# A decoder step on one core: its startup rewritten, with half-size loads on two queues, sample rows over all partitions, and a pinned order

## The chip, the cores and the metric

The kernel runs on one core of one Trainium2 chip. The metric is device time in microseconds (us). Three timed runs of the kernel before gave 1955.08, 1953.29 and 1950.29 us, median 1953.29. One more execution was taken with the profiler, and its trace is what is read here. The engines are named as the profile names them: PE (TensorE matmul), PEld (its weight load), DVE (VectorE), ACT (ScalarE), POOL (GpSimd) and SP (SyncE, which here only issues DMAs). `ACTq`, `SPq` and `PEq` are the instruction queues of those engines.

## What is computed

One inference step of a hybrid decoder layer, for 256 prompt tokens and 64 sample tokens (8 sequences of 8) that share all weights. Everything is float32:

```python
h = rmsnorm(x) * norm_mix_w                     # x: 320 tokens x 2048
proj = h @ w_in                                 # q, k, v, gates of two branches
x = x + (sig(gate_a) * (mlstm(proj) @ w_branch_a)
         + sig(gate_b) * (gla(proj) @ w_branch_b)) @ w_out
h2 = rmsnorm(x) * norm_ffn_w
u, g = h2 @ ffn_w_up, h2 @ ffn_w_gate
x = x + (gelu(conv3(u)) * g) @ ffn_w_down
y = rmsnorm(x) * final_norm_w                   # and the new recurrent states
```

The change touches only the first line, and the part of the second that makes q and k of the first two GLA heads.

## The kernel before

All activations stand transposed, features on the 128 partitions and the 320 tokens along the free dimension, so that a product is `[256 columns of w]^T @ h^T` in two PSUM tiles of 128x320. The weights are the stationary operand. A float32 product is done in three passes of the type float32r: a weight block `raw` is split into `wh` (a rounded copy, ACT, line 69) and `wl = raw - wh` (DVE, line 70), the activation likewise into `hH` and `hL`, and `mm3` (lines 74 to 76) adds wh·hH, wh·hL and wl·hH. Weight blocks are 512 KB (four row tiles by 256 columns); the pool `ring` keeps four `raw` and three each of `wh` and `wl`, so the loads run ahead of PE by a few blocks. PSUM holds four tiles with the tag `big` (products) and four with the tag `mx` (all else).

The startup, lines 131 to 219, makes h^T. `x_load(c)` brings 512 columns of x, one DMA for the prompt rows (512 KB) and one for the 64 sample rows (128 KB). `x_chunk(c)` transposes four feature tiles of 128 by the identity on PE (three transposes each: two blocks of prompt tokens and one of sample tokens, line 153), and evacuates each to hH (ACT, line 154), hL (DVE, line 155) and xT (lines 158 and 160), a plain copy that is written to DRAM by POOL (line 161) for the residual later. The norm's weight `nmw` is multiplied in there. The norm's scale per token is not: `token_scale` (lines 163 to 176) makes it apart. ACT squares the rows of x, one instruction for each block of tokens, and sums them (line 168), DVE divides by 2048 (169), POOL raises to the power -1/2 (170), DVE spreads each column over 128 (`lh`, 174), PE transposes the spread columns (175), and DVE copies the result to `rstd_bc` (176), by which every product is scaled when it leaves PSUM (`evac_scaled`, line 129).

While the chunks arrive, PE already multiplies: the first products are q and k of two GLA heads (`gq_ps`, `gk_ps`), which use up all four `big` tiles. They go over the 16 feature tiles in four steps of four, one step for each chunk, 24 matmuls for gq and 24 for gk in a step, 192 together. Eight matmuls on a tile of ones (line 110) run ahead of everything. Three transposes of small vectors (`vrow`, lines 215 to 217) follow, and then the product of the gates and all the others.

The order of the instructions on each engine isn't that of the code: `schedule_with_timeline_sim=True` lets a scheduler place them, engine by engine, when the program is built. Each engine then works through its list in that order and waits at each instruction for what it needs. DMAs wait in the same way, on SP's and ACT's queues: each load shares one of eight semaphores with the load issued eight before it, and is not issued before that one has landed.

## Time and profile before

| | us |
|---|---|
| timed runs | 1950.29 to 1955.08, median 1953.29 |
| span of the profiled execution | 1950.9 |
| PE busy in it | 1930.5 |
| first transposes of x on PE | 5.16 |
| first product matmul | 9.75 |
| first matmul after gq, gk and the vrow transposes | 48.31 |

The table's last three lines are starts of rows of the timeline, counted from the start of the span. "Busy" counts an engine from the start to the modelled end of its instructions, also where matmuls lie close behind each other and overlap; a busy PE may still be working slowly, so the pace is read from the starts of its matmuls. In an answer on waits, a row names who waited, for what, and for how long in total, how often, and at the longest. A row of the windows gives, for each engine, busy us and the number of instructions, then PE's granted clock (1.00 is full speed), the share of the DMA engines that was busy and the GB/s.

### The profile page before, as it was taken

To read this page: it belongs to the slowest core of one execution; us is meant where nothing else is said; L and a number is where in the kernel's file an instruction comes from. 1 tells how busy PE (TensorE), PEld (TensorE's weight loads), DVE (VectorE), ACT (ScalarE), POOL (GpSimd) and SP (SyncE) were. 2 spreads that over 40 slices of the span, in tenths; PEclk is the share of its full clock that TensorE was granted. 3 is DMA by queue.
4 is the path that set the end of the run, shared out by engine and by line. 5 is a ranking of instruction groups with operands and counts; after the bars stand their busy time and mean duration, and the time that the engine had idled before them with its cause. 6 is when DMAs were issued, how large, how long until landed. Compare 5 with 4: busy or idle time off the path is not lost.

```text
span 1950.9 us, 32725 instructions
## 1 busy us (share of the span) xinstructions
PE 1930.5 (99%) x13190; PEld 1908.9 (98%) x13190; DVE 1107.0 (57%) x1658; ACT 811.4 (42%) x1096; POOL 332.6 (17%) x618
## 2 busy tenths in 40 slices
PE   9999999999999999999999999999999999999997
PEld 8999999999999999999999999999999999999997
DVE  5767787878644444445655545554554555455455
ACT  5445444556533333333343324333432443343245
POOL 4221413143100000002211101110210120011014
PEclk9999999999999999999999999999999999999998
DMA  7745656575655555556444444444444444444442
GB/s 235 196 130 172 200 167 205 164 218 150 200 156 149 147 150 151 151 152 205 149 146 154 147 149 151 152 152 151 143 151 151 151 152 151 151 148 150 148 151 95
DMA packets 300224, 311.63 MB, mean 160 GB/s; under 512 B 15264, under 2 KB 292026, under 8 KB 300073
## 3 DMA queue, kind: packets, MB, share of 16 engines
q1 hardware_dynamic: 287849, 283.53, 48.0%
q0 software_dynamic: 7328, 24.50, 3.7%
q8 instruction: 103, 1.69, 0.4%
q10 hardware_dynamic: 4896, 1.52, 0.3%
q14 instruction: 48, 0.39, 0.1%
HBM read 287.03 MB, written 22.48 MB: 159 GB/s over the span
## 4 chain that ended last, share of the span: by engine, by line


## 5 line engine op out<-in xcount | busy, mean ns | idle before, releaser
L70 DVE TENSOR_TENSOR wl<-raw,wh 128x1024 fp32r<-128x1024 f32 x504 | 628.1, 1246 | 623.3 <-ACT wh L69 621.5
L69 ACT ACTIVATE wh<-raw 128x1024 fp32r<-128x1024 f32 x504 | 533.9, 1059 | 852.2 <-PE big L75 725.9
L74 PE MATMUL big<-hH,wh 128*128 128x320 f32 x2832 | 879.5, 311 | 2.5 <-ACT wh L69 2.5
L76 PE MATMUL big<-hH,wl 128*128 128x320 f32 x2832 | 879.6, 311 | 0.0
L75 PE MATMUL big<-hL,wh 128*128 128x320 f32 x2832 | 878.7, 310 | 0.0
L74 PEld LDWEIGHTS big<-hH,wh 128*128 128x128 f32 x2832 | 532.8, 188 | 3.5 <-ACT wh L69 2.6
L76 PEld LDWEIGHTS big<-hH,wl 128*128 128x128 f32 x2832 | 532.8, 188 | 1.4 <-issue 0.4
L75 PEld LDWEIGHTS big<-hL,wh 128*128 128x128 f32 x2832 | 532.8, 188 | 0.9 <-issue 0.4
L75 PE MATMUL big<-aL,wh 128*128 128x320 f32 x704 | 217.9, 310 | 0.0
L76 PE MATMUL big<-aH,wl 128*128 128x320 f32 x704 | 217.6, 309 | 0.0
L74 PE MATMUL big<-aH,wh 128*128 128x320 f32 x704 | 215.8, 309 | 0.0
L76 PEld LDWEIGHTS big<-aH,wl 128*128 128x128 f32 x704 | 132.4, 188 | 0.0
L75 PEld LDWEIGHTS big<-aL,wh 128*128 128x128 f32 x704 | 132.4, 188 | 0.0
L74 PEld LDWEIGHTS big<-aH,wh 128*128 128x128 f32 x704 | 131.8, 188 | 0.0
L876 POOL COPY conv<-u 128x2 f32<-128x2 f32 x44 | 8.2, 187 | 527.5 <-DVE u L873 527.5
L75 PE MATMUL big<-mL,wh 128*128 128x320 f32 x256 | 78.8, 309 | 0.0
L74 PE MATMUL big<-mH,wh 128*128 128x320 f32 x256 | 78.7, 309 | 0.0
L76 PE MATMUL big<-mH,wl 128*128 128x320 f32 x256 | 78.7, 309 | 0.0
L807 POOL TENSOR_TENSOR g<-g 128x320 f32<-128x320 f32 x16 | 14.6, 915 | 353.8 <-DVE g L803 353.8
L914 DVE TENSOR_TENSOR x<-big,x 128x320 f32<-128x320 f32 x96 | 46.6, 488 | 45.7 <-PE big L76 45.6
L888 POOL TENSOR_TENSOR g<-g,uc 128x256 f32<-128x256 f32 x44 | 32.6, 741 | 211.8 <-DVE g L887 211.8
L75 PE MATMUL big<-yL,wh 128*128 128x320 f32 x192 | 59.2, 308 | 0.0
(363 smaller groups left out, 1933.5 us busy)
## 6 DMA issues: line engine op xcount, KB each, us to landing
raw<-in_w_in SPq DMA_DIRECT2D x176, 512.0 KB, 3.7
raw<-in_ffn_w_up SPq DMA_DIRECT2D x88, 512.0 KB, 3.6
raw<-in_ffn_w_gate SPq DMA_DIRECT2D x88, 512.0 KB, 3.6
raw<-in_ffn_w_down SPq DMA_DIRECT2D x88, 512.0 KB, 3.5
raw<-in_w_out SPq DMA_DIRECT2D x32, 512.0 KB, 3.5
C<-in_state_mlstm_C SPq DMA_DIRECT2D x32, 256.0 KB, 6.4
o_C_s<-C POOLq DMA_DIRECT2D x32, 256.0 KB, 3.6
raw<-in_w_branch_a SPq DMA_DIRECT2D x16, 512.0 KB, 3.4
```

The costliest lines, as they stand in the source:

```text
L69: nc.scalar.activation(hi, raw, AF.Copy)
L70: nc.vector.tensor_tensor(lo, raw, hi.bitcast(F32), op=ALU.subtract)
L74: nc.tensor.matmul(out, wh, xh, start=first, stop=False)
L75: nc.tensor.matmul(out, wh, xl, start=False, stop=False)
L76: nc.tensor.matmul(out, wl, xh, start=False, stop=last)
L807: nc.gpsimd.tensor_tensor(sg[m], sg[m], acc[m], op=ALU.add)
L876: nc.gpsimd.tensor_copy(conv1[:, 0:2, c], u[:, T:T + 2])
L888: nc.gpsimd.tensor_tensor(g[:, 0:T], g[:, 0:T], gel[m][:, 0:T], op=ALU.mult)
L914: nc.vector.tensor_tensor(x2[k], pt[:, :N], x2[k], op=ALU.add)
```

## The change

Only the startup is rewritten; of the rest, comments go and `id2` is made earlier.

- Loads. x comes in pieces of 2, 2, 4, 4 and 4 feature tiles for the prompt rows (256 or 512 KB). The first gq and gk weight blocks come in two halves of 256 KB each, in an order that alternates with x. The sample rows come in eight DMAs of 64 KB, each for a pair of feature tiles: the first tile of the pair lies on partitions 0 to 63 and the second on 64 to 127 (`xs`). Four of those eight go through ACT's queue, all else through SP's. `norm_mix_w` (`nmr`) moves from ACT's queue to SP's, second in line.
- Work. A tile's transposes are again three, the third reads `xs` with a 64-row piece of the identity. Splits and products of the first step are done by halves (`rows_split`, `rows_product`). Within a piece the products now go pass by pass: all wh·hH, then all wh·hL, then all wl·hH, where before the three passes of one feature tile followed each other.
- Token scale. The sample rows are squared as 128 half rows of 1024, and the two halves of a token are added on PE with `id2`, two stacked identities, which is a new matmul with a DVE copy behind it. `id2` therefore moves from the mixers' masks to the constants.
- Order. `pin` (`keep_in_program_order`) holds the pinned instructions of each engine in the order of the code; the rest is still placed by the scheduler. With the code's order, `token_scale` comes behind the last tiles' evacuation, between the last 24 matmuls of gq and the last 24 of gk.

```diff
+    pin = tc.keep_in_program_order
...
     nc.gpsimd.memset(epsc, EPS)
     onec = cp.tile([P, 1], F32, name="onec")
     nc.vector.memset(onec, 1.0)
+    id2 = cp.tile([P, 64], F32, name="id2")
+    nc.gpsimd.tensor_tensor(id2, ident[:, 0:64], ident[:, 64:128], op=ALU.add)
     mhalf = cp.tile([P, 3], F32, name="mhalf")
     nc.gpsimd.memset(mhalf, -0.5)
     warm = cp.tile([P, 1], F32, name="warm")
-    nc.scalar.activation(warm, onec, AF.Copy)
     pw = mx("mx0")
     for _ in range(NWARM):
         nc.tensor.matmul(pw[:, 0:P], ones, ones, start=True, stop=True)
...
     def evac_scaled(dst, pt, scale):
         nc.vector.scalar_tensor_tensor(dst, pt[:, :N], scale, rstd_bc, op0=ALU.mult, op1=ALU.mult)
     with tc.tile_pool(name="st", bufs=1) as st:
         vrow = st.tile([P, 3, P], F32, name="vrow")
         nmr = st.tile([16, P], F32, name="nmr")
-        nc.scalar.dma_start(nmr, a["norm_mix_w"].rearrange("o (k p) -> (o k) p", p=P))
         nmw = st.tile([P, 16], F32, name="nmw")
-        pv = mx("mx1")
-        nc.tensor.transpose(pv[:, :16], nmr, ident[0:16, 0:16])
-        nc.vector.tensor_copy(nmw, pv[:, :16])
-        xn = st.tile([P, 3, DM], F32, name="xn")
-        def x_load(c):
-            cs = slice(c * 512, (c + 1) * 512)
-            nc.sync.dma_start(xn[:, 0:2, cs], a["x_prompt"][0].rearrange("(b p) c -> p b c", p=P)[:, :, cs])
-            nc.sync.dma_start(xn[0:64, 2, cs], a["x_sample"].rearrange("b t c -> (b t) c")[:, cs])
-        def x_chunk(c):
-            xT = st.tile([P, 4, N], F32, name=f"xT{c}")
-            for kk in range(4):
-                k = c * 4 + kk
+        xn = st.tile([P, 2, DM], F32, name="xn")
+        xs = st.tile([P, NK // 2, P], F32, name="xs")
+        xT = [st.tile([P, 4, N], F32, name=f"xT{c}") for c in range(4)]
+        def x_load(k0, nk):
+            cs = slice(k0 * P, (k0 + nk) * P)
+            nc.sync.dma_start(xn[:, :, cs], a["x_prompt"][0].rearrange("(b p) c -> p b c", p=P)[:, :, cs])
+        def xs_load(eng, *pairs):
+            src = a["x_sample"].rearrange("b t (k i c) -> i (b t) k c", i=2, c=P)
+            for k in pairs:
+                eng.dma_start(xs[:, k:k + 1], src[:, :, k:k + 1])
+        def x_tiles(k0, nk):
+            pts = []
+            for k in range(k0, k0 + nk):
                 pt = mx("mx2")
-                for j, (t0, tn) in enumerate(TOK):
-                    nc.tensor.transpose(pt[:, t0:t0 + tn], xn[:tn, j, k * P:(k + 1) * P], ident[:tn, :tn])
-                nc.scalar.activation(hH[k], pt[:, :N], AF.Copy, scale=nmw[:, k:k + 1])
-                nc.vector.scalar_tensor_tensor(hL[k], pt[:, :N], nmw[:, k:k + 1], hH[k].bitcast(F32),
-                                               op0=ALU.mult, op1=ALU.subtract)
-                if kk % 2:
-                    nc.scalar.copy(xT[:, kk], pt[:, :N])
+                r = slice(64 * (k % 2), 64 * (k % 2) + 64)
+                for j in range(2):
+                    pin(nc.tensor.transpose(pt[:, j * P:(j + 1) * P], xn[:, j, k * P:(k + 1) * P], ident))
+                pin(nc.tensor.transpose(pt[:, T:N], xs[r, k // 2], ident[r, r]))
+                pin(nc.scalar.activation(hH[k], pt[:, :N], AF.Copy, scale=nmw[:, k:k + 1]))
+                pin(nc.vector.scalar_tensor_tensor(hL[k], pt[:, :N], nmw[:, k:k + 1], hH[k].bitcast(F32),
+                                                   op0=ALU.mult, op1=ALU.subtract))
+                pts.append((k, pt))
+            return pts
+        def x_keep(pts):
+            for k, pt in pts:
+                if k % 2:
+                    pin(nc.scalar.copy(xT[k // 4][:, k % 4], pt[:, :N]))
                 else:
-                    nc.vector.tensor_copy(xT[:, kk], pt[:, :N])
-            nc.gpsimd.dma_start(xT_d[c], xT)
+                    pin(nc.vector.tensor_copy(xT[k // 4][:, k % 4], pt[:, :N]))
+                if k % 4 == 3:
+                    nc.gpsimd.dma_start(xT_d[k // 4], xT[k // 4])
         def token_scale():
             junk = st.tile([P, DM], F32, name="junk")
             rs = st.tile([P, 3], F32, name="rs")
             nc.gpsimd.memset(rs, 1.0)
-            for j, (t0, tn) in enumerate(TOK):
-                nc.scalar.activation(junk[:tn], xn[:tn, j], AF.Square, accum_out=rs[:tn, j:j + 1])
+            for j in range(2):
+                pin(nc.scalar.activation(junk, xn[:, j], AF.Square, accum_out=rs[:, j:j + 1]))
+            pin(nc.scalar.activation(junk[:, 0:DM // 2], xs.rearrange("p k c -> p (k c)"), AF.Square,
+                                     accum_out=rs[:, 2:3]))
+            pr = mx("mx3")
+            nc.tensor.matmul(pr[0:64, 0:1], id2, rs[:, 2:3], start=True, stop=True)
+            nc.vector.tensor_copy(rs[0:64, 2:3], pr[0:64, 0:1])
             nc.vector.tensor_scalar(rs, rs, 1.0 / DM, EPS, op0=ALU.mult, op1=ALU.add)
             nc.gpsimd.tensor_tensor(rs, rs, mhalf, op=ALU.pow)
             pr = mx("mx3")
...
         gq_ps = [big(), big()]
         gk_ps = [big(), big()]
-        def first(c0, c):
-            return weights(w_in[4 * c * P:4 * (c + 1) * P, c0:c0 + 256], 4, 2)
-        x_load(0)
-        wq = first(C_GQ, 0)
-        x_load(1)
-        wkk = first(C_GK, 0)
-        x_chunk(0)
-        for c in range(4):
-            if c < 2:
-                x_load(c + 2)
+        def blocks(c):
+            t = []
+            for c0, out in ((C_GQ, gq_ps), (C_GK, gk_ps)):
+                raw = ring.tile([P, 4, 256], F32, tag="raw", name="raw", bufs=RAW)
+                hi = ring.tile([P, 4, 256], F32R, tag="wh", name="wh", bufs=3)
+                lo = ring.tile([P, 4, 256], F32R, tag="wl", name="wl", bufs=3)
+                t.append((c, c0, out, raw, hi, lo))
+            return t
+        def rows_in(blk, i, n):
+            c, c0, out, raw, hi, lo = blk
+            r0 = (4 * c + i) * P
+            nc.sync.dma_start(raw[:, i:i + n], w_in[r0:r0 + n * P, c0:c0 + 256].rearrange("(k p) c -> p k c", p=P))
+        def rows_split(blk, i, n):
+            c, c0, out, raw, hi, lo = blk
+            pin(nc.scalar.activation(hi[:, i:i + n], raw[:, i:i + n], AF.Copy))
+            pin(nc.vector.tensor_tensor(lo[:, i:i + n], raw[:, i:i + n], hi[:, i:i + n].bitcast(F32), op=ALU.subtract))
+        def rows_product(blk, i, n):
+            c, c0, out, raw, hi, lo = blk
+            for ps_, (w, x) in enumerate(((hi, hH), (hi, hL), (lo, hH))):
+                for m in range(2):
+                    for kk in range(i, i + n):
+                        k = 4 * c + kk
+                        pin(nc.tensor.matmul(out[m][:, :N], w[:, kk, m * P:(m + 1) * P], x[k],
+                                             start=(k == 0 and ps_ == 0), stop=(k == NK - 1 and ps_ == 2)))
+        xs_load(nc.scalar, 0)
+        pin(nc.scalar.activation(warm, onec, AF.Copy))
+        x_load(0, 2)
+        nc.sync.dma_start(nmr, a["norm_mix_w"].rearrange("o (k p) -> (o k) p", p=P))
+        b0, b1 = blocks(0)
+        rows_in(b0, 0, 2)
+        rows_in(b1, 0, 2)
+        x_load(2, 2)
+        xs_load(nc.scalar, 1)
+        rows_in(b0, 2, 2)
+        rows_in(b1, 2, 2)
+        x_load(4, 4)
+        xs_load(nc.scalar, 2, 3)
+        n0, n1 = blocks(1)
+        rows_in(n0, 0, 4)
+        rows_in(n1, 0, 4)
+        x_load(8, 4)
+        xs_load(nc.sync, 4, 5)
+        pv = mx("mx1")
+        pin(nc.tensor.transpose(pv[:, :16], nmr, ident[0:16, 0:16]))
+        pin(nc.vector.tensor_copy(nmw, pv[:, :16]))
+        pts = x_tiles(0, 2)
+        rows_split(b0, 0, 2)
+        rows_split(b1, 0, 2)
+        rows_product(b0, 0, 2)
+        x_keep(pts)
+        pts = x_tiles(2, 2)
+        rows_product(b1, 0, 2)
+        rows_split(b0, 2, 2)
+        rows_split(b1, 2, 2)
+        x_keep(pts)
+        rows_product(b0, 2, 2)
+        pts = x_tiles(4, 2)
+        rows_product(b1, 2, 2)
+        x_keep(pts)
+        for c in range(1, 4):
+            b0, b1 = n0, n1
+            rows_split(b0, 0, 4)
+            pts = x_tiles(4 * c + 2, 2)
+            rows_split(b1, 0, 4)
+            if c == 1:
+                x_load(12, 4)
+                xs_load(nc.sync, 6, 7)
             if c < 3:
-                x_chunk(c + 1)
-            if c == 3:
+                n0, n1 = blocks(c + 1)
+                rows_in(n0, 0, 4)
+                rows_in(n1, 0, 4)
+            rows_product(b0, 0, 4)
+            x_keep(pts)
+            if c < 3:
+                pts = x_tiles(4 * c + 4, 2)
+                rows_product(b1, 0, 4)
+                x_keep(pts)
+            else:
                 token_scale()
-            part_product(gq_ps, w_in, C_GQ, 4 * c, NK, hH, hL, wq)
-            part_product(gk_ps, w_in, C_GK, 4 * c, NK, hH, hL, wkk)
-            if c < 3:
-                wq, wkk = first(C_GQ, c + 1), first(C_GK, c + 1)
+                rows_product(b1, 0, 4)
         gq, gk = (mg.tile([P, 2, N], F32, tag=t, name=t) for t in ("gq", "gk"))
         for m in range(2):
             evac_scaled(gq[:, m], gq_ps[m], DK ** -0.5)
...
-        id2 = mc.tile([P, 64], F32, name="id2")
-        nc.gpsimd.tensor_tensor(id2, ident[:, 0:64], ident[:, 64:128], op=ALU.add)```

What this makes of the engines' lists is shown at three places. First PE, from the first transposes on. A name's number tells tiles apart: hH_101 to hH_116 (before) and hH_102 to hH_117 (after) are the 16 feature tiles in order, hL likewise. Before:

```order
L153 MATMUL mx_168<-ident,xn 128x128 x2
L153 MATMUL mx_175<-ident,xn 128x128 x2
L153 MATMUL mx_168<-ident,xn 128x64
L153 MATMUL mx_175<-ident,xn 128x64
L153 MATMUL mx_182<-ident,xn 128x128 x2
L153 MATMUL mx_182<-ident,xn 128x64
L153 MATMUL mx_189<-ident,xn 128x128 x2
L153 MATMUL mx_189<-ident,xn 128x64
L74 MATMUL big<-hH_101,wh 128x320
L75 MATMUL big<-hL_117,wh 128x320
```

After:

```order
L160 MATMUL mx_186<-ident,xn 128x128 x2
L161 MATMUL mx_186<-ident,xs 128x64
L160 MATMUL mx_192<-ident,xn 128x128 x2
L161 MATMUL mx_192<-ident,xs 128x64
L226 MATMUL big<-hH_102,wh 128x320
L226 MATMUL big<-hH_103,wh 128x320
L226 MATMUL big<-hH_102,wh 128x320
L226 MATMUL big<-hH_103,wh 128x320
L226 MATMUL big<-hL_118,wh 128x320
```

The first product stood behind the transposes of four tiles and now stands behind those of two. Second, ACT, where it squares the rows of x (`junk,rs<-xn`). Before, in the third step of four:

```order
L158 COPY xT_199<-mx_221 128x320
L168 ACTIVATE junk,rs<-xn 128x2048
L154 ACTIVATE hH_110<-mx_299,nmw 128x320
L154 ACTIVATE hH_111<-mx_306,nmw 128x320
L69 ACTIVATE wh<-raw 128x1024
L168 ACTIVATE junk,rs<-xn 128x2048
L154 ACTIVATE hH_112<-mx_313,nmw 128x320
```

After, from the last weight block but one (`graw` is the raw block of the gates):

```order
L217 ACTIVATE wh<-raw 128x1024
L162 ACTIVATE hH_116<-mx_468,nmw 128x320
L162 ACTIVATE hH_117<-mx_474,nmw 128x320
L217 ACTIVATE wh<-raw 128x1024
L404 ACTIVATE wh<-graw 128x8x4 x2
L404 ACTIVATE wh<-graw 128x8x16
L171 COPY xT_148<-mx_474 128x320
L182 ACTIVATE junk,rs<-xn 128x2048
L404 ACTIVATE wh<-graw 128x8x4 x2
L404 ACTIVATE wh<-graw 128x8x16
L182 ACTIVATE junk,rs<-xn 128x2048
L183 ACTIVATE junk,rs<-xs 128x1024
```

The first two squares stood ahead of hH_110 and hH_112, six and four tiles before the last, and now stand behind the last tile, hH_117, and behind the split of the gates' weights. Third, PE, where it takes up the token scale. Before:

```order
L74 MATMUL big<-hH_113,wh 128x320
L75 MATMUL big<-hL_129,wh 128x320
L175 MATMUL mx_479<-ident,lh_480 128x128
L175 MATMUL mx_479<-ident,lh_483 128x128
L175 MATMUL mx_479<-ident,lh_486 128x64
L76 MATMUL big<-hH_113,wl 128x320
L74 MATMUL big<-hH_114,wh 128x320
```

After (the first two rows end gq's last step, and the last begins gk's):

```order
L226 MATMUL big<-hH_116,wl 128x320
L226 MATMUL big<-hH_117,wl 128x320
L186 MATMUL mx_515<-rs,id_78 64x1
L194 MATMUL mx_520<-ident,lh_521 128x128
L301 MATMUL mx_571<-ident,vrow 128x52
L302 MATMUL mx_571<-ident,vrow 128x88
L303 MATMUL mx_571<-ident,vrow 128x88
L194 MATMUL mx_520<-ident,lh_524 128x128
L194 MATMUL mx_520<-ident,lh_527 128x64
L226 MATMUL big<-hH_114,wh 128x320
```

The token scale stood inside the last step, behind two of its matmuls; it now stands behind 24 of them, with the new matmul on `rs` ahead of it and the vrow transposes inside it, and gk's last 24 matmuls stand behind it all. Behind these the gates' product follows in both. In the mixers that come later the scheduler has placed some instructions differently, with no edit there; from the output gates on PE's list is the same.

1 line of the change is left out of this document (removed).

## The prediction

> **What bounds the kernel now.** I read the page first, then the windows of the first and the worst stretches, then the waits of PE, then PE's timeline. The page says that PE works nearly all the time:
>
> ```profile
> span 1950.9 us, 32725 instructions
> PE 1930.5 (99%) x13190; PEld 1908.9 (98%) x13190; DVE 1107.0 (57%) x1658; ACT 811.4 (42%) x1096; POOL 332.6 (17%) x618
> ```
>
> PE stands idle for 1950.9 - 1930.5 = 20.4 us in all, so no change of order can be worth more than that, plus what PE does at a low clock. The windows place the loss (us, then busy us and number of instructions per engine, then granted clock, DMA share, GB/s):
>
> ```profile
> 0.00:5.00 5.00, 3.56 (x17) 3.35 (x17) 0.35 (x3) 1.49 (x2) 4.09 (x24) 1.00 0.50 155
> 5.00:10.00 5.00, 2.36 (x14) 1.54 (x14) 1.22 (x3) 1.89 (x3) 2.74 (x13) 1.00 1.05 311
> 10.00:15.00 5.00, 4.88 (x23) 4.51 (x23) 4.75 (x8) 3.16 (x7) 0.57 (x1) 0.66 1.08 317
> 100.00:150.00 50.00, 47.89 (x325) 46.43 (x324) 31.63 (x75) 22.11 (x34) 11.75 (x21) 0.97 0.48 142
> 1900.00:1951.00 51.00, 39.13 (x283) 38.47 (x281) 26.81 (x51) 28.29 (x70) 22.57 (x26) 0.89 0.30 96
> ```
>
> Some 4 us are lost in the first 10 us, 2 in the mixers around 100 us and 12 in the tail. The waits of PE up to 100 us say for what the startup waits, and the third row here, from the waits over all the span, is the worst of the mixers:
>
> ```profile
> PE big L74 <- ACT wh L69: 2.5, 1, 2.5
> PE mx L153 <- DMA xn<-in_x_prompt: 0.5, 1, 0.5
> PE mx L576 <- DVE AT L579: 3.0, 2, 1.9
> ```
>
> The 2.5 us are the wait for the first weight block, 512 KB, which lands late and is split late. PE's timeline (start, us, engine, line, names; [idle before]) gives the pace and the milestones:
>
> ```profile
> 5.16 2.11 PE L153 MATMUL mx<-ident,xn 128*128 128x128 f32 x12 [0.47 <-DMA xn<-in_x_prompt]
> 9.75 0.41 PE L74 MATMUL big<-hH,wh 128*128 128x320 f32 x1 [2.48 <-ACT wh L69]
> 11.67 0.47 PE L74 MATMUL big<-hH,wh 128*128 128x320 f32 x1
> 14.07 0.39 PE L75 MATMUL big<-hL,wh 128*128 128x320 f32 x1
> 21.80 1.15 PE L153 MATMUL mx<-ident,xn 128*128 128x128 f32 x6
> 22.88 0.42 PE L74 MATMUL big<-hH,wh 128*128 128x320 f32 x1
> ...
> 40.11 0.97 PE L175 MATMUL mx<-ident,lh 128*128 128x128 f32 x6
> 41.01 0.41 PE L76 MATMUL big<-hH,wl 128*128 128x320 f32 x1
> ...
> 47.71 0.31 PE L76 MATMUL big<-hH,wl 128*128 128x320 f32 x1
> 47.95 0.26 PE L215 MATMUL mx<-ident,vrow 52*128 52x52 f32 x1
> 48.31 0.39 PE L74 MATMUL big<-hH,wh 128*128 128x320 f32 x1
> ...
> 55.28 0.31 PE L76 MATMUL big<-hH,wl 128*128 128x320 f32 x1
> 59.98 0.31 PE L75 MATMUL big<-hL,wh 128*128 128x320 f32 x1
> ```
>
> From 55.28 to 59.98 there are 32 steps, so a matmul costs 4.70 / 32 = 0.147 us at full clock. From 11.67 to 14.07 there are nine steps of 0.267 us: that is the stretch with the granted clock of 0.66, and it cost 9 x 0.12 = 1.1 us, with its beginning some 1.3. Two tiles' transposes take 22.88 - 21.80 = 1.08, one tile 0.54. The token scale takes 41.01 - 40.11 = 0.90, with no wait ahead of it; the vrow transposes 48.31 - 47.71 - 0.15 = 0.45.
>
> My milestone is 48.31, the first matmul behind gq and gk. What comes behind it has the same work in both kernels, so what the change makes is the shift of this point, plus what a new order does to the waits in the mixers.
>
> **The change part by part.** First the part that gains, with the rows of PE's head start and of ACT's first steps:
>
> ```profile
> 1.12 3.40 PE L110 MATMUL mx<-ones 128*128 128x128 f32 x16 [1.12 <-DVE onec L102]
> 22.42 1.10 ACT L154 ACTIVATE hH<-mx,nmw 128x320 fp32r<-128x320 f32 x2
> 31.42 1.06 ACT L69 ACTIVATE wh<-raw 128x1024 fp32r<-128x1024 f32 x1
> 32.38 1.36 ACT L154 ACTIVATE hH<-mx,nmw 128x320 fp32r<-128x320 f32 x3
> ```
>
> The first tile's transposes start at 5.16 now, when 512 KB have landed; a piece of half that size lands between 4.5 (the eight matmuls on ones end at 1.12 + 3.40 = 4.52) and 5.2, and I take 4.9. The piece of the sample rows comes in beside it on ACT's queue. That `nmr` is now second on SP, and PE's first transpose waits for it, can cost up to 0.4 us and lies in the same bounds. From the transposes to the first product, ACT sets the time: hH starts 22.42 - 21.80 = 0.62 behind the transposes, two of them take 1.0, and a split of half a block about half of 32.38 - 31.42 = 0.96, so 0.5: 4.9 + 0.62 + 1.0 + 0.5 = 7.0. I take 7.3, since the half block may land late: at worst it comes as late as the whole block does now (9.75), at best PE starts at 6.7. From there PE has 192 matmuls (28.2), 14 tiles (7.6), the token scale (0.90), vrow (0.45) and the new matmul on `rs` (0.15): 37.3 in all, and without any wait gk would end at 44.6, that is 3.7 us earlier than 48.31.
>
> The pass order within a piece has the same count of matmuls and costs nothing at the pace of 0.147; wl is needed later by eight matmuls, which hides its split (DVE). The eight sample DMAs instead of four, and the waits of SP for a load issued eight before, I cost at 0.15: up to 15 us the DMA engines are full (311 and 317 GB/s), and every piece has about a microsecond of slack. At the start of each of the last three steps the products stand directly behind the transposes whose hH they need, third and fourth in line: hH of the second tile ends at 0.62 + 1.0 = 1.6 behind the transposes' start and is wanted at about 1.4, so 0.25 each, 0.75. `id2` and the table load have no one waiting for them. The scaled squares of the sample rows, 1024 long instead of 2048, save ACT about 0.85.
>
> Now the part that loses. The squares stood between earlier tiles' work on ACT, and PE took up the result at 40.11 without a wait. Now they stand behind the last tile, and PE stands still at the matmul on `rs` until they are done; gk's last 24 matmuls are queued behind it, and behind these the rest of the kernel. The rows of the chain are these:
>
> ```profile
> 24.37 1.91 ACT L168 ACTIVATE junk<-xn 128x2048 f32<-128x2048 f32 x1
> 26.26 0.52 ACT L154 ACTIVATE hH<-mx,nmw 128x320 fp32r<-128x320 f32 x1
> 31.09 0.43 ACT L158 COPY xT<-mx 128x320 f32<-128x320 f32 x1 [0.93 <-DVE rs L169]
> 40.88 0.55 ACT L321 ACTIVATE wh<-graw 128x32 fp32r<-128x32 f32 x3 [1.90 <-POOL wh L318]
> 30.27 0.17 DVE L169 TENSOR_SCALAR rs<-rs 128x3 f32<-128x3 f32 x1 [0.74 <-ACT junk L168]
> 30.52 0.89 POOL L170 TENSOR_TENSOR rs<-rs,mhalf 128x3 f32<-128x3 f32 x1 [7.21 <-DVE rs L169]
> 31.45 0.68 DVE L174 TENSOR_SCALAR lh<-ones,rs 128x128 f32<-128x128 f32 x3 [1.01 <-POOL rs L170]
> ```
>
> Count from the start of the last two tiles' transposes. ACT: the two hH end at 1.6; the split of gk's last block until 2.6 (0.96); three small splits of graw 0.45; a copy 0.33; a square 26.26 - 24.37 = 1.89; three splits 0.45; a square 1.89; the short square 1.05. That is 8.7. Then PE's matmul with its way there and back 0.35, two DVE steps of 0.17 with gaps 0.45, POOL's power 0.9 and the first `lh` 0.3: PE goes on at 10.7. Its matmuls of gq end at 1.1 + 24 x 0.147 + 0.15 = 4.8. PE stands still for 10.7 - 4.8 = 5.9; it is not hidden, since all that PE has left behind this point is behind it in line. I take 6.0. Bounds: 5.0 if the graw splits and copies overlap better than these rows, 7.5 if graw's own load, or the two memsets of POOL (0.95 each) that ACT and the power stand behind, come late.
>
> The clock comes on top. The one slow stretch now follows a gap of 2.48 us behind 2.11 us of transposes. A gap of 6 us should bring another, between none and twice the present one with a longer tail (0 to 3.0); I take one and a half times 1.3, 1.9. The startup's own may stay or go (0 to 1.7): 1.0. The Trainium skill, "TensorE: Matmul & The Clock Gate", Part 1 (the HAM clock gate), says that the clock is halved behind an idle window of about 3.4 us and comes back behind a busy one, with windows that run freely. By that rule the second stretch is near certain and lasts up to two windows, an estimate of 3.1 us at most; the present stretch, under 3.4 us long, agrees.
>
> Sum: 44.6 + 0.15 + 0.75 + 6.0 + 1.9 + 1.0 = 54.4, against 48.31: 6.1 us later. The mixers' new order I take at 0, between -3 (the 3.0 us of L576 go) and +4 (they double). The span would be 1957.0; the median of the runs is 2.4 above the span, within their spread of 4.8, and 1953.3 + 6.1 gives 1959.4.
>
> A measurement of this kernel can tell 0.3%, 5.9 us, from no change, so faster is below 1947.4 and slower above 1959.2. My forecast lies just at the upper edge.
>
> **The rivals.** *The squares are covered* (0.13): if PE does not in fact stand still there, the startup keeps its 3.7 us less the small waits and one slow stretch, 44.6 + 0.9 + 1.0 = 46.5, or 1.8 earlier: 1951.5, not slower. For it speaks that ACT is only 42% busy. Against it stands the list: all of ACT's 8.7 us follow the last tile, and PE has 3.5 us of work there. It decides from the point where ACT's squares end before PE ends gq, 4.8 behind the transposes, and they would have to be 4 us shorter.
>
> *The stall spreads* (0.12): the pieces land as late as the blocks do now, so that PE starts at 9.75 (2.5 more), or L576's waits double (3 more). Then it is 6.1 + 3 to 6, 1964 on average. For it speaks that the DMA engines are full from 5 to 15 us; against it, that the first half block has half as many bytes ahead of it.
>
> *The mixers' waits go* (0.05): the new order removes the 3.0 us at L576 and its slow stretch (clock 0.97 over 50 us, 1.5 us). With the stall it is 6.1 - 4.5, 1955; without, faster than 1947.
>
> **How the numbers follow.** The forecast case has 0.70, and with its own range of 4 to 8.5 us it lies on both sides of the edge, 0.37 slower and 0.33 the same. The first rival gives 0.12 same and 0.01 faster, the second 0.12 slower, the third 0.02 same and 0.03 faster. That makes 0.04 faster, 0.47 same, 0.49 slower. The low end is the sum of the forecast's low bounds, 44.6 - 0.6 + 5.0, with 0.9 of small waits and the mixers' -3, about 1952; the high end is the second rival's, 1966. Left out are the first rival's larger gains and what lies above.
>
> **What would show it.** PE's waits name DVE or ACT before the line of the new matmul and the first lh transpose, 5 to 7 us together; PE's first product starts near 7.3; gk ends near 54; the granted clock falls behind the stall. I am wrong in the main step if PE has no wait over 2 us there, wrong in the gain if the first product starts above 9, and wrong about the rest if the milestone and the end shift by different amounts.

## The result, and the profile after

| | kernel before | kernel after |
|---|---|---|
| median of the runs, us | 1953.41 (1950.29 to 1955.08, 4 runs) | 1964.51 (1964.08 to 1964.95, 4 runs) |
| profiled execution, us | span 1950.9 | 1964.95, span 1963.1 |
| first product matmul | 9.75 | 8.78 |
| first matmul behind gq and gk | 48.31 | 62.55 |

The change makes the kernel slower: the ratio is 1.0061, with a 95% interval of 1.0047 to 1.0075. The forecast was 1959.4 within 1952 to 1966, so the sign and the range hold, and the point is 5 us too low. The shift of 11.1 us lies outside the 4 to 8.5 us of the forecast case itself; the stated range holds it only because its upper end was taken from a rival. The milestone moved by 14.2 us, the span by 12.2, so what lies behind the milestone, mainly the mixers, gave 2 us back.

The page of the kernel after has nearly the same work on every engine; what grew is the span:

```profile
span 1963.1 us, 32735 instructions
PE 1936.4 (99%) x13192; PEld 1912.7 (97%) x13192; DVE 1106.5 (56%) x1661; ACT 809.3 (41%) x1096; POOL 332.2 (17%) x618
```

PE's waits over all its span, the largest first:

```profile
PE mx L186 <- issue: 3.8, 1, 3.8
PE big L226 <- ACT wh L217: 3.2, 2, 2.1
PE mx L194 <- DVE lh L193: 1.9, 1, 1.9
PE mx L659 <- DVE AT L662: 1.8, 1, 1.8
PE mx L786 <- POOL ds L784: 1.5, 1, 1.5
...
PE mx L161 <- DMA xs<-in_x_sample: 0.6, 1, 0.6
```

L186 is the new matmul on `rs`, and L194 the transposes of `lh` right behind it: together 5.7 us, the stall that was forecast. The first names "issue", that is, no releaser that the profile shows; the timeline further down shows whom PE waits for. L226, the products of gq and gk, has a wait of 2.1 us that was not forecast.

PE's timeline (start, us, engine, line, names, count; [idle before]):

```profile
8.78 1.43 PE L226 MATMUL big<-hH,wh 128*128 128x320 f32 x4 [1.14 <-ACT wh L217]
10.01 1.27 PE L226 MATMUL big<-hL,wh 128*128 128x320 f32 x4
11.08 1.27 PE L226 MATMUL big<-hH,wl 128*128 128x320 f32 x4
...
13.72 0.86 PE L226 MATMUL big<-hH,wh 128*128 128x320 f32 x4
...
33.25 2.54 PE L226 MATMUL big<-hH,wh 128*128 128x320 f32 x8 [2.07 <-ACT wh L217]
35.59 2.09 PE L226 MATMUL big<-hL,wh 128*128 128x320 f32 x8
37.52 1.34 PE L226 MATMUL big<-hH,wl 128*128 128x320 f32 x8
38.69 0.38 PE L160 MATMUL mx<-ident,xn 128*128 128x128 f32 x2
...
47.18 1.34 PE L226 MATMUL big<-hH,wl 128*128 128x320 f32 x8
52.33 0.34 PE L186 MATMUL mx<-rs,id 128*64 128x1 f32 x2 [3.82 <-issue]
54.58 0.77 PE L194 MATMUL mx<-ident,lh 128*128 128x128 f32 x2 [1.90 <-DVE lh L193]
...
57.14 2.50 PE L226 MATMUL big<-hH,wh 128*128 128x320 f32 x8
59.44 2.10 PE L226 MATMUL big<-hL,wh 128*128 128x320 f32 x8
...
62.55 0.31 PE L75 MATMUL big<-hH,wh 128*128 128x320 f32 x1
```

Read the pace from starts, not from the "us" column. From 10.01 the next four start 1.07 later, 0.267 each: half clock. From 13.72 on they run at full clock again, 24 of them until 17.35, 0.15 each. Three stretches run at half clock: 8.78 to 13.7, 33.25 to about 37.5 (24 products take 38.69 - 33.25 = 5.44, of which 3.9 would do), and 54.58 to about 61, behind the stall.

What PE waits for in the stall stands in the timeline of all engines:

```profile
46.71 1.92 ACT L182 ACTIVATE junk<-xn 128x2048 f32<-128x2048 f32 x1
...
49.05 1.90 ACT L182 ACTIVATE junk<-xn 128x2048 f32<-128x2048 f32 x1
...
51.08 1.06 ACT L183 ACTIVATE junk<-xs 128x1024 f32<-128x1024 f32 x1
...
53.22 0.89 POOL L189 TENSOR_TENSOR rs<-rs,mhalf 128x3 f32<-128x3 f32 x1 [3.42 <-DVE rs L188]
```

The squares end at 52.1, the matmul on `rs` follows at 52.33, POOL's power at 54.1, the first transpose at 54.58. The last product of gq would have been followed by another at 47.18 + 8 x 0.147 = 48.36.

The unforeseen wait begins on SP's queue. Its issues (the second column is how long it took to issue):

```profile
1.81 0.93 SPq L213 DMA_DIRECT2D raw<-in_w_in  x2
6.33 0.37 SPq L147 DMA_DIRECT2D xn<-in_x_prompt  x1
...
20.16 3.32 SPq L152 DMA_DIRECT2D xs<-in_x_sample  x2
23.60 3.28 SPq L213 DMA_DIRECT2D raw<-in_w_in  x2
```

and what SP waited for:

```profile
SPq L147 <- DMA xs<-in_x_sample: 5.1, 2, 3.6
...
SPq L152 <- DMA xs<-in_x_sample: 3.5, 1, 3.5
```

From 2.74 to 6.33 SP issues nothing: the next prompt piece waits for a sample piece on ACT's queue to land. The third step's two weight blocks go out only at 23.60, behind the last sample pieces, and PE wants them at 31. The windows show what the DMA engines did meanwhile (columns as before; DMA share and GB/s last):

```profile
0.00:5.00 5.00, 3.88 (x17) 3.65 (x17) 0.17 (x2) 1.49 (x2) 4.09 (x24) 1.00 0.49 73
10.00:15.00 5.00, 5.00 (x23) 4.17 (x23) 2.22 (x5) 1.95 (x5) 0.87 (x3) 1.00 0.95 285
20.00:25.00 5.00, 5.00 (x32) 4.21 (x31) 3.73 (x6) 3.39 (x6) 2.46 (x4) 1.00 0.47 144
100.00:150.00 50.00, 48.22 (x340) 46.37 (x339) 33.69 (x84) 25.18 (x41) 16.59 (x27) 1.00 0.52 135
```

From 20 to 25 us, while SP waits for sample pieces, the DMA engines were busy for 0.47 of the time. The first 5 us moved 73 GB/s where the kernel before moved 155, at the same share (0.49 and 0.50), so there the share alone says nothing; from 4 to 5 us, within SP's pause, it is 0.31 at 33 GB/s. The last row is the mixers': a clock of 1.00 where it was 0.97 before.

### The profile page after: what moved, and what is told of

Read it like the earlier page. It is cut to its first block, busy times and chain, and to the rows that moved or that the text cites. A ratio compares the mean times of both kernels' runs of the same rounds, so it can differ in the third digit from the quotient of the medians.

```text
span 1963.1 us, 32735 instructions
## 1 busy us (share of the span) xinstructions
PE 1936.4 (99%) x13192; PEld 1912.7 (97%) x13192; DVE 1106.5 (56%) x1661; ACT 809.3 (41%) x1096; POOL 332.2 (17%) x618
## 3 DMA queue, kind: packets, MB, share of 16 engines
q8 instruction: 103, 1.69, 0.4%
## 4 chain that ended last, share of the span: by engine, by line
## 5 line engine op out<-in xcount | busy, mean ns | idle before, releaser
L71 DVE TENSOR_TENSOR wl<-raw,wh 128x1024 fp32r<-128x1024 f32 x496 | 620.0, 1250 | 617.0 <-ACT wh L70 616.1
L70 ACT ACTIVATE wh<-raw 128x1024 fp32r<-128x1024 f32 x496 | 526.1, 1061 | 842.6 <-PE big L76 723.4
L75 PE MATMUL big<-hH,wh 128*128 128x320 f32 x2768 | 859.1, 310 | 0.0
L76 PE MATMUL big<-hL,wh 128*128 128x320 f32 x2768 | 859.0, 310 | 0.0
L77 PE MATMUL big<-hH,wl 128*128 128x320 f32 x2768 | 857.5, 310 | 0.0
L77 PEld LDWEIGHTS big<-hH,wl 128*128 128x128 f32 x2768 | 519.8, 188 | 0.9 <-issue 0.4
L75 PEld LDWEIGHTS big<-hH,wh 128*128 128x128 f32 x2768 | 519.8, 188 | 0.9 <-issue 0.4
L76 PEld LDWEIGHTS big<-hL,wh 128*128 128x128 f32 x2768 | 519.8, 188 | 0.8
L76 PE MATMUL big<-aL,wh 128*128 128x320 f32 x704 | 217.9, 310 | 0.0
L75 PE MATMUL big<-aH,wh 128*128 128x320 f32 x704 | 215.8, 309 | 0.0
L76 PEld LDWEIGHTS big<-aL,wh 128*128 128x128 f32 x704 | 132.4, 188 | 0.0
L75 PEld LDWEIGHTS big<-aH,wh 128*128 128x128 f32 x704 | 131.8, 188 | 0.0
L76 PE MATMUL big<-mL,wh 128*128 128x320 f32 x256 | 78.8, 309 | 0.0
L75 PE MATMUL big<-mH,wh 128*128 128x320 f32 x256 | 78.7, 309 | 0.0
L77 PE MATMUL big<-yH,wl 128*128 128x320 f32 x192 | 59.2, 308 | 0.0
```

What stands on the lines that cost most here:

```text
L70: nc.scalar.activation(hi, raw, AF.Copy)
L71: nc.vector.tensor_tensor(lo, raw, hi.bitcast(F32), op=ALU.subtract)
L75: nc.tensor.matmul(out, wh, xh, start=first, stop=False)
L76: nc.tensor.matmul(out, wh, xl, start=False, stop=False)
L77: nc.tensor.matmul(out, wl, xh, start=False, stop=last)
```

## The experiments

Three theories stand against each other. Theory 1 is the prediction's: the stall at the token scale, and the half clock behind it. Theory 2: the sample pieces hold SP's queue, and what is loaded behind them comes late. Theory 3: the half clock of the startup is a loss of its own. Every ratio is to runs of the kernel before on the same chip, whose median lay between 1951.95 and 1953.44; 0.001 is 2 us.

| | change to | ratio | interval | median less before's, us | milestone | span |
|---|---|---|---|---|---|---|
| after | | 1.0061 | 1.0047 to 1.0075 | 11.1 | 62.55 | 1963.1 |
| e4, two more squares | after | 1.0072 | 1.0057 to 1.0087 | 13.9 | 66.36 | 1965.2 |
| e5, busy in the stall | after | 1.0043 | 1.0029 to 1.0056 | 8.2 | 58.79 | 1959.1 |
| e3, not pinned | after | 1.0049 | 1.0034 to 1.0064 | 9.1 | 55.95 | 1958.1 |
| e2, samples on POOL | after | 1.0043 | 1.0027 to 1.0060 | 8.9 | 61.77 | 1962.1 |
| e1, squares early | after | 1.0027 | 1.0017 to 1.0036 | 5.7 | 53.23 | 1954.1 |
| e13, samples in four | e1 | 1.0009 | 1.0000 to 1.0018 | 2.4 | 50.90 | 1951.5 |
| e6, samples with prompt | e1 | 1.0013 | 1.0004 to 1.0022 | 2.1 | 48.46 | 1953.8 |
| e7, busy at the start | e1 | 1.0028 | 1.0018 to 1.0038 | 5.2 | 56.08 | 1957.5 |
| e11, third block on POOL | e7 | 1.0011 | 1.0002 to 1.0020 | 2.1 | 52.23 | 1951.3 |
| e10, both | e6, e7 | 1.0002 | 0.9993 to 1.0011 | 0.6 | 47.57 | 1952.2 |
| e12, squares spread | e10 | 0.9994 | 0.9985 to 1.0003 | -1.2 | 47.60 | 1948.0 |
| e14, kept busy | before | 0.9995 | 0.9986 to 1.0004 | -1.2 | 47.42 | 1947.5 |

Milestone and span are of the profiled execution. Differences between kernels below are of the fifth column.

**The stall: e4, e1, e5, e3.** e4 doubles the suspected cost; its two squares' sums are read by nothing.

```diff
             for j in range(2):
                 pin(nc.scalar.activation(junk, xn[:, j], AF.Square, accum_out=rs[:, j:j + 1]))
+            more = st.tile([P, 2], F32, name="more")
+            for j in range(2):
+                pin(nc.scalar.activation(junk, xn[:, j], AF.Square, accum_out=more[:, j:j + 1]))
```

> Two further squares of 2048 elements, whose sums nothing reads, stand in ScalarE's queue between the second square and the samples' square. Theory 1 (that chain is on the path): the wait in front of L186 grows from 3.8 by two times 1.9 to 7.6 us, and the time by 3.8 us, to 1968.3 (up to 1 us more if the slow clock behind it lasts longer). The rival (the chain is hidden, or given back later): under 1 us.

PE's timeline in e4:

```profile
56.07 0.34 PE L189 MATMUL mx<-rs,id 128*64 128x1 f32 x2 [9.80 <-issue]
```

PE came to this point 2.2 us earlier than in the kernel after (the third block's wait was absent in this execution), so the wait grew by more than the squares; PE went on at 56.07 instead of 52.33, 3.74 later, which is two squares. The milestone moved by 3.8, the span by 2.1, and the median by 2.8 where 3.8 was expected: the chain is on the path, and the mixers give a part back. The ratios' intervals overlap, so the time alone would not have settled it.

e1 moves the same three squares to places between the third step's work.

```diff
+            if c == 2:
+                square(0)
             rows_product(b0, 0, 4)
             x_keep(pts)
+            if c == 2:
+                square(1)
             if c < 3:
                 pts = x_tiles(4 * c + 4, 2)
                 rows_product(b1, 0, 4)
                 x_keep(pts)
+                if c == 2:
+                    square(2)
```

> The three squares of the token scale stand between the third block's work instead of behind the last two tiles; the sum across partitions on TensorE then stands right behind the last tiles, and the scale's transposes behind some eleven of gq's last products. Theory 1 (the changed kernel's stall at the token scale sits on the path, and a stretch of slow clock follows it): the 3.82 us in front of L186 goes, of the 1.90 us in front of L194 up to 1 us stays, and the slow products behind it (about 3 us) go: 8 to 9 us less than the changed kernel, 1955.5 to 1957, milestone (first product of the stage behind gq, gk and vrow) near 54 instead of 62.55. The rival (the stall is given back later, since the mixers wait for something else): the milestone moves and the time stays within 2 us of 1964.5. Under both, the 2.07 us in front of the third block's products stays.

PE's timeline in e1:

```profile
17.89 0.76 PE L230 MATMUL big<-hL,wh 128*128 128x320 f32 x4
...
32.85 1.69 PE L230 MATMUL big<-hH,wh 128*128 128x320 f32 x8
...
46.20 0.46 PE L198 MATMUL mx<-ident,lh 128*128 128x128 f32 x2 [0.96 <-DVE lh L197]
```

Of the stall 0.96 us is left, the 24 products behind it take 3.62 us, full clock, and the profiled execution is 9.0 us shorter than the kernel after's. Its time, 1955.9, is that of two runs in nine, though; the other seven lie at 1958.6 to 1959.5. Theory 1 gets its full price in the trace and 5.4 us in the median. In the trace PE found the third block ready at 32.85, since the half clock lasted to 17.9 instead of 13.7 and had made PE late by itself. That the seven longer runs are those in which the clock came up sooner and PE waited for that block is likely after e7 (below), which lies at the same time, but of those runs there is no trace.

e5 leaves the stall and fills it with products that nothing reads.

```diff
             pr = mx("mx3")
+            for _ in range(17):
+                pin(nc.tensor.matmul(pr[:, P:2 * P], ones, ones, start=True, stop=True))
             nc.tensor.matmul(pr[0:64, 0:1], id2, rs[:, 2:3], start=True, stop=True)
...
             nc.gpsimd.tensor_tensor(rs, rs, mhalf, op=ALU.pow)
+            for _ in range(7):
+                pin(nc.tensor.matmul(pr[:, P:2 * P], ones, ones, start=True, stop=True))
```

> The changed kernel with 24 further products of ones by ones, which nothing reads, on TensorE inside the stall: 17 in front of the sum across partitions, 7 between it and the scale's transposes (3.6 and 1.5 us at 0.21 each at full clock). Theory 1 with the clock: TensorE counts as busy, the granted clock stays up, and the products behind the stall run at 0.147 instead of 0.267: the first product of the next stage comes 3 us earlier than 62.55, the time falls by about 3 us to 1961.5. The rival (the slow products come from something else, such as the load on the DMA engines): the products behind stay at 0.267 and the time stays at 1964.5 or rises by up to 1 us.

In e5's timeline the products behind the scale run at full clock, eight in 56.45 - 55.17 = 1.28 where the kernel after took 2.30:

```profile
55.17 1.43 PE L230 MATMUL big<-hH,wh 128*128 128x320 f32 x8
56.45 1.34 PE L230 MATMUL big<-hL,wh 128*128 128x320 f32 x8
```

The median fell by 2.9, as expected: work of no use, on an engine that is waiting, is worth 2.9 us.

e3 takes the pinned order away.

```diff
-    pin = tc.keep_in_program_order
+    pin = lambda i: i
```

> The pinned order is taken away and all else kept: the scheduler then sets the order, with the squares ahead of the last tiles' copies. Theory 1: the stall of 3.8 + 1.9 us at the token scale and the slow clock behind it go, 8 to 9 us less than the changed kernel, and the 2.07 us in front of the third block (SyncE's queue, which the pinned order doesn't touch) stays: 1955 to 1957. The rival (the pinned order keeps TensorE fed elsewhere, so taking it away opens other waits): 1960 to 1968, with new waits in front of the tiles' transposes or L226.

The stall is gone from the waits of e3, as theory 1 has it, but two waits of 1.8 us came in front of the tiles, and one of 1.6 us ahead of the milestone:

```profile
PE mx L160 <- DMA xn<-in_x_prompt: 1.8, 1, 1.8
PE mx L160 <- ACT xT L171: 1.8, 1, 1.8
```

So the rival's price applies too: most of what the scheduler's order saves at the squares it loses at other places, and a gain of 2.0 us is left. That the place of the three squares in the pinned order makes the stall is shown by e1, which changes it alone.

**SP's queue: e2, e6, e13.** e2 was meant to free SP by sending all sample pieces through GpSimd.

```diff
-                eng.dma_start(xs[:, k:k + 1], src[:, :, k:k + 1])
+                nc.gpsimd.dma_start(xs[:, k:k + 1], src[:, :, k:k + 1])
```

> The eight sample pieces are issued by GpSimd's queue alone. Theory 2 (the sample pieces hold SyncE's queue through shared semaphores, 5.1 and 3.5 us in its waits, so the third block's weights and the first pieces come late): SyncE's waits for xs go, the third block's wait of 2.07 us and the slow products behind it (1.9 us) go, 4 to 5 us less than the changed kernel, about 1960; the first product (8.78) comes up to 1.5 us earlier if the first sample piece lands earlier. The rival (the DMA engines are full anyway, 0.74 to 0.95 busy in these stretches): something else comes late in its place, 0 to 1 us. A third possibility: GpSimd's queue starts later than ScalarE's, the first sample piece lands later than 6.36 and the first product moves back by the difference. The stall at the token scale stays in all of them.

SP's waits for xs went, and 2.2 us with them where 4 to 5 were expected (the intervals overlap), but it tells less than it was meant to. The first sample piece landed later, the third possibility, and the first product moved from 8.78 to 9.02. SP now issued the ten small vector loads ahead of the third step's blocks, five of them waiting 1.1 to 2.6 us for an earlier load, and the blocks went out no sooner than in the kernel after:

```profile
25.36 3.02 SPq L213 DMA_DIRECT2D raw<-in_w_in  x4
```

PE still waited 1.28 us for them, so what a free queue is worth stays open here. e6 builds on e1 and loads the sample rows as the kernel before did.

```diff
-                pin(nc.tensor.transpose(pt[:, T:N], xs[r, k // 2], ident[r, r]))
+                pin(nc.tensor.transpose(pt[:, T:N], xn[0:64, 2, k * P:(k + 1) * P], ident[0:64, 0:64]))
...
-        def xs_load(eng, *pairs):
...
+            nc.sync.dma_start(xn[0:64, 2, cs], a["x_sample"].rearrange("b t c -> (b t) c")[:, cs])
```

> The kernel with early squares (e1), and the sample rows as before the change: 64 rows by 256 or 512 columns in xn, one piece with each prompt piece, all on SyncE's queue; five sample loads instead of eight, no sum across partitions, the third square 2048 long on 64 rows. Theory 2 (the small sample pieces on two queues hold SyncE's queue, and all that is loaded behind comes late): in the first 5 us the DMA engines move about 150 GB/s as before the change instead of 73 to 80, the third block has no wait, the first product starts at 7.3 or earlier; 3 to 4 us less than e1, about 1955.5. The rival (the engines are full anyway, and what is left against before is the slow clock in the first 18 us): within 1 us of e1, 1958 to 1960.

SP's queue and PE in e6:

```profile
15.09 2.46 SPq L207 DMA_DIRECT2D raw<-in_w_in  x2
```

```profile
7.09 0.97 PE L220 MATMUL big<-hH,wh 128*128 128x320 f32 x4 [1.14 <-ACT wh L211]
```

The blocks go out 8.3 us sooner than in e1 (23.40), the first product starts 1.2 us sooner, and the median falls by 3.6 us. The first 5 us moved 125 GB/s instead of 80. This undoes the layout together with the number of loads, and e13 parts them: the layout of the change, in four loads.

```diff
-        def xs_load(eng, *pairs):
-            src = a["x_sample"].rearrange("b t (k i c) -> i (b t) k c", i=2, c=P)
-            for k in pairs:
-                eng.dma_start(xs[:, k:k + 1], src[:, :, k:k + 1])
+        def xs_load(k0, k1):
+            for i in range(2):
+                src = a["x_sample"].rearrange("b t (k i c) -> i (b t) k c", i=2, c=P)[i]
+                nc.scalar.dma_start(xs[64 * i:64 * i + 64, k0:k1], src[:, k0:k1])
...
-        xs_load(nc.scalar, 0)
+        xs_load(0, 2)
...
-        xs_load(nc.scalar, 1)
+        xs_load(2, 8)
```

> The kernel with early squares (e1) and its sample layout, but the sample rows in four loads instead of eight, all issued early on ScalarE's queue: two of 64 rows by 256 columns, two of 64 rows by 768. Theory 2 in its narrow form (it is the number of loads that share a few semaphores with SyncE's queue, not the layout): SyncE's waits for xs behind 10 us go, the third block's loads are issued near 15 instead of 23.4, its wait goes; 1.5 to 3.5 us less than e1, about 1956. SyncE's first wait for xs (3.0 us) can stay, since four loads still stand ahead of its second prompt piece. The rival (the layout over 128 partitions, in runs of 512 bytes, is slow by itself): within 1 us of e1.

SP's queue and PE in e13:

```profile
3.92 0.37 SPq L147 DMA_DIRECT2D xn<-in_x_prompt  x1
...
16.32 1.72 SPq L217 DMA_DIRECT2D raw<-in_w_in  x2
```

```profile
29.00 1.69 PE L230 MATMUL big<-hH,wh 128*128 128x320 f32 x8
```

The blocks go out at 16.32, PE takes them up at 29.00 without a wait, and the median falls by 3.3 us. The bytes and their places in `xs` are those of e1, so the rival on the layout falls. The narrow form of theory 2, that the number of loads is what costs, is not shown by it, though. By the expectation SP's first wait could stay, since four loads still stand ahead of the second prompt piece; it nearly went, and this piece goes out at 3.92 where it went out at 5.75 in e1. Beside the number, e13 changes the queue (all on ACT's) and the form of a load: in the change one load takes both tiles of a pair, the two halves of the partitions as its outermost step, in e13 each half has loads of its own. The sample pieces came in faster with it. These are the rows of ACT's queue (packets, MB, share of the 16 DMA engines' time) between 3 and 5 us, in the kernel after and then in e13:

```profile
q10 hardware_dynamic: 100, 0.05, 10.3%
q10 hardware_dynamic: 375, 0.18, 32.3%
```

10.3% of 16 engines is 1.6 engines at a time, 32.3% is 5.2. So what e13 shows is that the sample pieces of the change are slow to land, and that what waits for them on SP's queue waits long. Which of the three differences makes them slow stays open: no run changes one of them alone. Nor is all of the 3.3 us the block's: in the executions that were profiled, e13's products ran at full clock from the first (7.78), e1's at half until 17.9.

**The clock at the start: e7, e11, e10, e12, e14.** e7 puts four idle products into the gap ahead of the first real one.

```diff
         pts = x_tiles(0, 2)
+        pw = mx("mx1")
+        for _ in range(4):
+            pin(nc.tensor.matmul(pw[:, 0:P], ones, ones, start=True, stop=True))
```

> The kernel with early squares (e1), and 4 products of ones by ones, which nothing reads, between the second tile's transposes and the first product, where TensorE waits 1.7 us (4 times 0.42 at half clock). Theory 3 (what is left of the loss is the half clock from 8.3 to 13.7 or 17.9, since the gap ahead of the first product counts as idle): the clock is up at the first product or some 3 us behind it, 2 to 4.5 us less than e1, about 1955.5. The rival (the clock's window runs freely and the gap isn't what decides, or the time is lost again in the wait for the third block, which lands at about 31 whatever TensorE does): within 1 us of e1.

PE's timeline in e7:

```profile
8.40 0.85 PE L230 MATMUL big<-hH,wh 128*128 128x320 f32 x4 [0.48 <-ACT wh L221]
...
11.65 0.44 PE L160 MATMUL mx<-ident,xn 128*128 128x128 f32 x2 [1.23 <-DMA xn<-in_x_prompt]
...
33.19 2.54 PE L230 MATMUL big<-hH,wh 128*128 128x320 f32 x8 [2.95 <-ACT wh L221]
```

The clock is up from the first product on, PE is through with the tiles ahead of the third block 2.7 us sooner than in e1, and waits there 2.95 us, with another stretch at half clock behind. Only 0.5 us is gained: the block lands when it lands, which was the rival. By itself this would read as if the clock didn't matter. e11 takes this block off SP's queue.

```diff
-            nc.sync.dma_start(raw[:, i:i + n], w_in...)
+            (nc.gpsimd if c == 2 else nc.sync).dma_start(raw[:, i:i + n], w_in...)
```

> The kernel e7 (early squares, sample pieces as in the change, TensorE kept busy at the start), with the third block's two weight loads on GpSimd's queue instead of SyncE's. In e7 these loads are issued at 23.4, behind the sample pieces, and TensorE waits 2.95 us for them and then runs 24 products at half clock (2.9 us more). Theory 2 (they come late since SyncE's queue is held, not since the engines are full): they are issued near 15 to 17, the wait and the slow products go, the time is 4.5 to 6 us less than e7's 1958.6, about 1953.3. The rival (the engines are full before 20 us, at 0.80 to 0.90: what lands earlier there makes the last prompt pieces late): the wait turns up in front of the tiles' transposes instead, under 1.5 us less.

The queue of POOL and PE's timeline in e11:

```profile
15.00 0.82 POOL L217 DMA_DIRECT2D raw<-in_w_in  x1 [5.16 <-DVE wl L222]
```

```profile
11.67 0.44 PE L160 MATMUL mx<-ident,xn 128*128 128x128 f32 x2 [1.30 <-DMA xn<-in_x_prompt]
...
12.81 1.42 PE L230 MATMUL big<-hH,wh 128*128 128x320 f32 x4
...
31.74 1.69 PE L230 MATMUL big<-hH,wh 128*128 128x320 f32 x8
```

The wait is gone, and the median falls by 3.1 us; 4.5 to 6 were expected. What is missing is in the first two of these rows: the wait for the second prompt piece, which SP's first hold makes late, is still there as in e7 (1.30 and 1.23), and in this execution the clock fell behind it. So the third block's place behind the sample pieces in SP's line is what made it late.

e10 puts e6 and e7 together.

> Early squares, samples with the prompt as in e6, and the 4 products of e7 together. If theories 2 and 3 are both right, neither the third block's wait nor the half clock is left, and the stage ends near 46 to 48, before the 48.31 of the kernel before: 1950 to 1953. If only the clock counts, it is as e7; if only the queue counts, as e6.

The stage ends at 47.57, 0.74 ahead of the kernel before's, with the clock at full speed from the first product. The time is the one before's: on top of e6 the idle products are worth 1.5 us of the median, with intervals that overlap; the longest run fell from 1959.9 to 1955.1, the shortest did not. e12 spreads the squares further.

```diff
             if c == 2:
-                square(0)
+                square(1)
...
-                if c == 2:
-                    square(2)
+                if c < 3:
+                    square(2 * c - 2)
```

> The kernel e10 with the three squares spread further: the first behind the second block's products, the second within the third block, the samples' one as before. In e10 ScalarE is full from 30 to 40 us (4.5 and 4.8 of 5 us) and TensorE waits 0.78 us for the last block's split. If that wait is on the path it goes: 0.5 to 0.8 us less than e10's 1954.1, 1953.4. The rival: a square before the third block makes its split late instead, 0 to 1 us more.

The median fell by 1.8, with intervals that overlap, and not for the reason given: the wait of 0.78 went, and yet the milestone is where it was (47.60), since the first product started 0.2 us later, and the scale's transposes wait a little. The span shrank by 4.2 us, in the mixers: their two longest waits, for POOL `ds` and DVE `AT`, are 2.3 and 2.0 us in e10 and 0.2 and 1.1 in e12, and the granted clock from 100 to 150 us is 0.97 in e10 and 1.00 in e12, which is some 1.5 us of the 50. Why the mixers wait less there no run here tells apart. e14 asks whether the idle products would have helped the kernel before the change too.

```diff
                 nc.scalar.activation(hH[k], pt[:, :N], AF.Copy, scale=nmw[:, k:k + 1])
+                if k == 0:
+                    for _ in range(4):
+                        nc.tensor.matmul(gk_ps[1][:, 384:384 + P], ones, hH[k].bitcast(F32)[:, 0:P], start=True, stop=True)
```

> The kernel before the change, with 4 products that nothing reads (ones by the first hH, 128 columns) on TensorE in its 2.48 us gap ahead of the first product. Theory 3 (the half clock follows the gap): the nine products at 0.267 and their beginning, 1.3 us, go; 1 to 1.5 us less than the kernel before, 1952. The rival: the clock falls or not by where its window stands, or the products push the first real one back: within 0.5 us, or up to 0.7 us more.

The clock came up at 11 instead of 14.3, with the first product 0.3 us later; the milestone came 0.9 us earlier, the median 1.2. The ratio's interval, 0.9986 to 1.0004, holds no change. e12 and e14 are the fastest kernels here, and neither can be told from the kernel before.

## Why the prediction was right, and where it was short

**The stall.** Forecast 6.0 us. From 48.36 to 54.58, less 0.15 for the matmul on `rs`, it is 6.1. The chain of rows taken from the trace of before was right row by row (ACT's squares end 8.7 behind the start of the last transposes, 43.40, as forecast), and e1, e4 and e5 show that it is on the path.

**The clock behind it.** Forecast 1.9, measured 2.8: the scale's transposes and the vrow rows take 57.14 - 54.58 = 2.56 against 1.51 in e1, and the 24 products 5.41 against 3.62. e5 gives back 2.9. The Trainium skill, "TensorE: Matmul & The Clock Gate", Part 1 (the HAM clock gate), by whose windows the prediction estimated at most 3.1, agrees with this stretch.

**The step that failed** is "The eight sample DMAs instead of four, and the waits of SP for a load issued eight before, I cost at 0.15", with the reason that the DMA engines are full up to 15 us. They were in the kernel before, from 5 us on; in the kernel after SP stands still until a sample piece has landed, these pieces land slowly, and in the first 5 us 73 GB/s were moved, in the next 236 (155 and 311 before). Its price is the third block's wait and half clock, 2.07 + 1.57 = 3.6 us in the profiled execution, and a part of the late first product. e13 and e11 give back 3.3 and 3.1 us. This term and the startup's half clock hide each other: in the executions of e1, e4 and e5 the half clock lasted to 17 or 18 us, PE came later, and the block's wait isn't there.

**The first product.** Forecast 7.3 within 6.7 to 9.75, measured 8.78: PE waited 0.6 us for the first sample piece, and then 1.1 us for the split of the half block. With the samples on SP's queue it is 7.09 (e6), with four loads on ACT's queue 7.78 and no wait for a sample piece (e13). So the 7.3 was right for the work; what it missed is how late the sample piece of the change lands, not ACT's queue as such. **The startup's own half clock.** Forecast 1.0, measured 2.0: 8.78 to 13.72 is 4.94, the same work in e10 takes 10.62 - 7.67 = 2.95.

**Small waits.** Forecast 0.75 and 0.15. With no half clock and one known wait of 0.78, e10's stage takes 47.57 - 7.67 = 39.9 against 37.15 of counted work, so what is left, put down to the waits for hH and hL, comes to 2.0. In the kernel after 1.9 is left for them: 1.5 + 1.0 + 3.6 + 0.1 + 0.9 + 1.0 is the whole difference of 8.1 between 54.4 and 62.55.

**The mixers.** Taken at 0 within -3 to +4, they gave 2.0 back; by the prediction's own sign, a milestone and an end that shift by different amounts, this part was wrong. PE's waits there add up to as much as before (1.8 + 1.5 + 0.8 us in the rows of L659, L786 and L530, against 3.0 + 0.8 in those of L576 and L447), but the granted clock from 100 to 150 us is 1.00 where it was 0.97, some 1.5 us. So of the third rival the slow stretch went and the waits did not. The span's shift less the milestone's is -0.4 to -3.8 in ten of the experiments, and +2.8 and +2.0 in e6 and e10, where the wait for POOL `ds` is the longest, 2.3 us; the mixers' part isn't settled better than that.

**The rivals.** "The squares are covered" fell with L186's wait. "The stall spreads" named 1964 and the time came out there, but not by its two ways: PE started at 8.78, not 9.75, and the mixers' waits didn't double. That the time lies within the range is in part luck: the number was right for a reason that was in no rival.

**Where the expected gain went.** Even with all of this mended, half-size pieces are worth 0.7 us of stage. Against the kernel before, e10 starts its first product 2.1 us sooner and has no half clock (1.3 us), but two tiles' transposes (1.08) that stood ahead of the first product now stand behind it, and the waits inside the stage are 2.75 us where the same sum for the kernel before, 48.31 - 9.75 - 1.3 - 28.2 - 12 x 0.54 - 1.35, leaves 1.2.

## What to carry to other kernels

Where an order is pinned, look for the instruction whose result the busiest engine takes up next, and count the whole list that stands ahead of it on the other engines; an engine that is 42% busy can still be the wait. A small load in a line that issues in order costs what it holds up, not its bytes: look at how long it takes to land, at what stands behind it, and at the bytes moved in the first microseconds. When one fix gains nothing, look for the next wait at the place where the gained time ends, before dropping it: e7 alone gained 0.5 us, and with e11 behind it 3.6.

## What the runs showed of the hardware

- Equal gaps do not bring equal clocks. Behind a wait of 1.23 us the products of e7 ran at full speed (12.80, four in 0.69), behind one of 1.30 at the same place those of e11 at half; the 0.96 us ahead of the scale's transposes was harmless in e1 and brought half clock in e13 (eight products in 2.30 from 43.99). The half clock at the start lasted 4.9 us in the kernel after and 9.6 in e1 with nearly the same list. The Trainium skill, "TensorE: Matmul & The Clock Gate", Part 1, lets the clock fall behind an idle window of about 3.4 us, with windows that run freely: that equal lists meet different clocks agrees with it, a fall behind gaps of 1 to 1.3 us does not, and the measurement decides. Even with the transposes beside the gap counted as idle, only 2.7 us lie between the products of e11, from 10.07 to 12.81.
- The granted clock of the windows is not always the pace: the kernel after shows 1.00 from 10 to 15 us, and its products there start every 0.267 us until 12.1; in e1 the same pace in the same window stands beside 0.50.
- The smaller load isn't the sooner one: the sample piece of 64 KB, issued on ACT's queue at 0.80, let its transpose start at 6.36, after 0.6 us of waiting, while the prompt piece of 256 KB, issued on SP's queue at the same time, was there for a transpose at 5.05. The loads of this form kept 1.6 of the 16 DMA engines busy at a time between 3 and 5 us, those of e13, of the same bytes in another form, 5.2.
